# Gate and up products with half of the tokens stationary and 512 weight columns moving

## The chip, the cores and the metric

The kernel runs on one core of one Trainium2 chip. The metric is the device time of one execution in microseconds (us), and the kernel before is given by three such times. Beside them stands one profiled execution, whose trace gives every instruction's start and duration on the core's engines: TensorE (PE, with its weight loads as PEld), VectorE (DVE), ScalarE (ACT), GpSimd (POOL), and the queue of SyncE (SP), which only issues transfers.

## What is computed

The reference is a causal trunk of two layers on 256 tokens of 1024 features in fp32. Each layer is a half-weighted SwiGLU block, a mixer, and another such block. The mixer is attention with pooling in layer 0 and a state-space layer (S5) with a gated linear unit (GLU) in layer 1. The four SwiGLU blocks (FFN 0 to 3) are what the change touches:

```
def _swiglu(h, w_gate, w_up, w_down):          # 1024 -> 2816 -> 1024
    return (jax.nn.silu(h @ w_gate) * (h @ w_up)) @ w_down

def reference(x, ...):
    for layer in range(2):
        x = x + 0.5 * _swiglu(_rmsnorm(x, ffn_norm[layer, 0]), ...)
        h = _rmsnorm(x, mix_norm[layer])
        x = x + (_even_mixer(h, ...) if layer % 2 == 0 else _odd_mixer(h, ...))
        x = x + 0.5 * _swiglu(_rmsnorm(x, ffn_norm[layer, 1]), ...)
    return x
```

## The kernel before

An fp32 product is made as three products in the type fp32r: high part by high part, high by low, low by high (`mm3`). The transposed, normed input of a block lies on chip as `hTh` and `hTl` (high and low, 8 tiles of 128 features by 256 tokens). Weights come from memory in pieces of 512 KB (tile `raw`, at most 4 on their way) and are split on chip: ACT rounds a piece to its high part (`wh`, `hi_of`, L176) and DVE subtracts that from the piece (`wl`, `tt`, L133). Two pieces make a unit, and 4 units have room at a time.

An FFN walks over 11 groups (`NG`) of 256 of its 2816 inner columns. Its units are ("g", f, g) for gate, ("u", f, g) for up, ("d", f, g) for down. For groups 1 to 10, `gate_up(f, g)` keeps a block of 128 weight columns stationary and moves all 256 tokens: 2 sides (gate, up) by 2 blocks of columns by 8 blocks of features by 3 products are 96 products of 256 columns. Their sums come out with the inner columns on the partitions, which is how the down products want them. So `sg` (Silu, ACT), `pr` (gate times up, DVE), `hh` (high, ACT) and `hl` (low, DVE), each of 128x512, follow straight on:

```
p = wk((128, 2, 256))
i = mm3(p[:, m], w[0][:, k, s], w[1][:, k, s], hTh[:, k], hTl[:, k], k == 0, k == 7)
```

Group 0 of each FFN is made in the head, beside the norm of the tokens' second half, by `gate_up_half`: half of the tokens (128) stationary, 256 weight columns of one side moving. There the sums have tokens on the partitions, so `hid_T` turns the result of a half with two transposes on TensorE (`tr`, 128x128 fp32, into a `sk` tile of PSUM) before `hh` and `hl` are made.

`down(f, g, t, c)` keeps 128 tokens of `hh` or `hl` stationary and moves 512 columns of the down weights, into `acc` tiles of PSUM; a group has 24 such products. `ffn_joint` runs the down products of group g - 1 behind the gate and up products of group g, and the last two groups' stand in `tail`. Outside a few stretches a scheduler, which works before the launch, lays down each engine's order; `prio(CHAIN)` prefers an instruction and `behind(...)` puts it behind others. The program is FFN 0, the mixer of layer 0, FFN 1, FFN 2, S5 with its GLU, FFN 3.

The tables of S5 are built by a generator (`s5_build`) on DVE beside the groups of FFN 1 and FFN 2; the names `X`, `E`, `b_q`, `b_pw`, `b_st` are its tiles. Four loads of 1 MB (`K`, units of kind "K") and four of 512 KB (`rawW`, kind "W") bring S5's maps back on chip when S5 begins, and 16 stores `V<-h` rearrange its input; all of these are issued by SP, in its order.

Of the kernel before, what the change touches and what calls it, by code (L numbers as in the profile page):

```python
# [25 lines left out]
RING = 4        # split units of weights on chip  # L26
RAW = 4         # pieces of weights on their way
CHAIN = 400     # the scheduler's preference for what TensorE waits for
WARM = 32       # products that nothing reads, before S5
WARM0 = 16      # and at the start  # L30
PACE = 0.8      # calls of the generators for a step
# the even mixer, call by call; digits: the half of the tokens and a part, for p the columns, the half (from 6 on of
# the columns, which come out turned) and the part
# h transposes of the input, p projections in, e rotary and rms of queries (0) or keys (1), T their transposes,
# s scores, x exponentials, t transposes of the weights, v values, V their transposes, g sums of windows,
# m their products, G their split, o projections out, l load of a vector
# [5 lines left out]
# S5, two of the eight jq at a time: f front (a copy of the input), u its transposes, w sums of the chunks,  # L42
# s scan, d direct part, o output; h0 transposes of the output's first half, x products that nothing reads
# [8 lines left out]
# columns of the constants: identity, masks of both halves, scales of the first sums of windows, places of d, frequencies  # L52
# [9 lines left out]
def shape_constants():  # L62
# [8 lines left out]
    # the patterns that hold a key, as the logarithm of their number (over the scale of the scores)  # L71
# [3 lines left out]
    # the first sums of a window of w hold fewer than w values  # L75
# [8 lines left out]
class InOrder:  # L84
    """an engine whose instructions keep the order of the program while strict is set"""
# [19 lines left out]
def trunk_kernel(ctx: ExitStack, tc: tile.TileContext, I, out):  # L105
# [19 lines left out]
    # pieces of weights on their way, units split, the step traced, calls due to the generators, units held back  # L125
    state = {"dma": 0, "split": 0, "step": 0, "credit": 0.0, "hold": False}

# [16 lines left out]
    def strict(on):  # L144
        """from here on TensorE keeps the order of the program, or no longer"""
        def f():
            PE.strict = on
        return f
# [17 lines left out]
    @contextmanager  # L166
    def behind(*names):
        """what is traced within is issued behind the instructions kept by these names, each on its engine"""
        with ExitStack() as st:
            for n in names:  # L170
                for i in pins.get(n, ()):
                    st.enter_context(tc.issue_after(i.ins))
            yield
# [20 lines left out]
    def unit_source(uid):  # L194
        kind = uid[0]
        if kind == "g":
            return cols_unit(I["ffn_w_gate"][uid[1] // 2, uid[1] % 2], uid[2])
        if kind == "u":
            return cols_unit(I["ffn_w_up"][uid[1] // 2, uid[1] % 2], uid[2])
# [6 lines left out]
        return cols_unit(I["s5_w_glu"][0], uid[1])  # L206

# [6 lines left out]
    def emit_dma(i):  # L214
# [10 lines left out]
        src, a, b = unit_source(units[i // 2])  # L225
        n = a // 2
        r = wraw.tile([128, n, b], F32, tag="raw", name="raw")
        keep("load", SP.dma_start(out=r, in_=src[:, (i % 2) * n:(i % 2 + 1) * n]))
        raws[i] = r

    def raw_busy(i):
        """whether the room that piece i takes still holds a piece of W"""
# [13 lines left out]
    def split_late():  # L246
        """from here on the low parts wait for split_now()"""
        nonlocal late
        late = []
# [9 lines left out]
    def emit_split(i):  # L259
# [18 lines left out]
        _, a, b = unit_source(units[i])  # L278
        h = wsp.tile([128, a, b], F32R, tag="wh", name="wh")
        l = wsp.tile([128, a, b], F32R, tag="wl", name="wl")  # L280
        n = a // 2
        for p in range(2):
            fill(2 * i + p)
            r = raws.pop(2 * i + p)
            s = slice(p * n, p * n + n)
            with behind(*(["split"] if i + p else ["norm"])):
                hi = hi_of(h[:, s], r)
                if late is None:
                    keep("splits", hi, tt(l[:, s], r, h[:, s].bitcast(F32), ALU.subtract))
                else:  # L290
                    late.append((l[:, s], r, h[:, s].bitcast(F32), ALU.subtract))
# [55 lines left out]
    def table(func, after="square"):  # L347
        """the table of a function, before its first use waits for it"""
# [23 lines left out]
    def split_T(t, kt0, ps):  # L372
        """PSUM [128, 4, 128] -> hi and lo of hT."""
# [13 lines left out]
    hid = {}  # L387

    def gate_up(f, g):
        wg, wu = held["g", f, g], held["u", f, g]  # L390
        ps = []
        for w in (wg, wu):
            p = wk((128, 2, 256))
            for m in range(2):
                for k in range(8):
                    s = slice(m * 128, (m + 1) * 128)
                    i = mm3(p[:, m], w[0][:, k, s], w[1][:, k, s], hTh[:, k], hTl[:, k], k == 0, k == 7)
            ps.append(p)
            if w is wg:
                keep("gate", i)  # L400
        sg = tmp.tile([128, 2, 256], F32, tag="t512", name="sg")
        pr = tmp.tile([128, 2, 256], F32, tag="t512", name="pr")
        h = hidp.tile([128, 2, 256], F32R, tag="hh", name="hh")
        l = hidp.tile([128, 2, 256], F32R, tag="hl", name="hl")
        with prio(CHAIN):
            ACT.activation(out=sg, in_=ps[0], func=AF.Silu)
            tt(pr, sg, ps[1], ALU.mult)
            hi_of(h, pr)
            tt(l, pr, h.bitcast(F32), ALU.subtract)
        hid[f, g] = (h, l)  # L410
# [5 lines left out]
    def gate_up_half(f, g, t, which, ks):  # L416
        w = held["gu"[which], f, g]
# [3 lines left out]
        p = gups[f, g, t][:, which]  # L421
        for x, y in ((hTh, w[0]), (hTh, w[1]), (hTl, w[0])):
            for k in ks:
                keep("gu", mm(p, x[:, k, o], y[:, k], k == 0 and y is w[0] and x is hTh, k == 7 and x is hTl))
        if which == 0 or ks[-1] != 7:
            return
        ps = gups.pop((f, g, t))
# [7 lines left out]
    def hid_T(f, g, t):  # L435
# [7 lines left out]
        with prio(CHAIN), behind("gate" if t else "gu"):  # L443
# [15 lines left out]
    cst = I["cst"]  # L459

# [1 line left out]
    at = {}  # L462

    def even_open():
# [18 lines left out]
        # values to pool and sums of windows, with room for the 8 zeros before the first  # L483
# [20 lines left out]
    def proj_in(c, t, ks):  # L504
        """the projections c of half t, or, where they are pooled, half t of their columns, turned"""
# [26 lines left out]
    def angle_tables(pool, ang, n, cos, sin, name):  # L532
        """cos and sin of ang [128, n]; quadrants by parts of pi / 2 that keep the products exact."""
# [41 lines left out]
        # u = 1 - o ; sin' = s * u + c * o ; cos' = c * u + s * o  # L575
# [670 lines left out]
    def ffn_joint(f, g0, g1, pend):  # L1246
        """groups g0 .. g1 - 1 of both halves; pend: calls that follow the first of them"""
        for g in range(g0, g1):
            paced.add(len(steps))
            S(lambda g=g: gate_up(f, g), ("g", f, g), ("u", f, g))  # L1250
            for fn in pend:
                S(fn)
# [295 lines left out]
```

## Time and profile before

| what | value |
|---|---|
| three runs | 957.85, 960.83, 962.18 us (median 960.83) |
| profiled execution, span from first to last instruction | 960.5 us |
| PE busy | 938.2 us, 98% of the span |
| weight loads (PEld) busy | 870.5 us, 91% |
| DVE busy | 640.9 us, 67% |
| ACT busy | 424.6 us, 44% |
| POOL busy | 58.3 us, 6% |
| mean granted TensorE clock | 0.994 of full speed |
| moved by DMA | 185.47 MB, mean 193 GB/s |

The profiled execution has no time of its own beside its span; the span is 0.33 us below the median of the three runs. Busy shares are means over stages that differ: DVE is lightly loaded in FFN 0 and full beside parts of FFN 1 and FFN 2. A matmul's duration in the trace holds its passage through the array, so consecutive ones overlap, and how long one holds the queue is the difference between two starts.

### The profile page before, as it was taken

The page shows a single profiled execution, that of the slowest core. Times are in us where ns is not written, and L with a number is a line of the kernel's source. Part 1 is how long each engine was busy: PE and PEld are TensorE (multiplying, and loading weights), DVE is VectorE, ACT ScalarE, POOL GpSimd, SP SyncE. Part 2 cuts the span into 40 slices and gives each one's busy share as a digit, 9 for nine tenths or more (in the row PEclk, how much of TensorE's full clock was granted, in tenths as well). Part 3 has the DMA queues.
Part 4 walks back from the last instruction along what each step waited for, and adds up shares of the span by engine and source line. Part 5 has one row for each costly group of instructions (what it writes and reads, how often), then busy time and mean ns, then how long its engine had stood idle before and what let it go on. Part 6 is the DMA issues. An engine that isn't in the chain of part 4 may idle for free.

```text
span 960.5 us, 17371 instructions
## 1 busy us (share of the span) xinstructions
PE 938.2 (98%) x7148; PEld 870.5 (91%) x7148; DVE 640.9 (67%) x1017; ACT 424.6 (44%) x563; POOL 58.3 (6%) x105
## 2 busy tenths in 40 slices
PE   8999999999998999999999999999879999999998
PEld 6999999989987999999999999999659999999997
DVE  5646654488866799997675898844586575554452
ACT  6534433455635443444454443442525364433440
POOL 0000000013020000013100340000000000000000
PEclk9999999999999999999999999999999999999999
DMA  8867666645477664679756696667656457666641
GB/s 246 267 192 227 191 178 198 187 139 163 144 160 221 191 190 147 195 244 298 236 187 181 161 275 182 194 196 249 217 198 208 143 162 218 192 177 195 181 149 44
DMA packets 146047, 185.47 MB, mean 193 GB/s; under 512 B 18896, under 2 KB 128400, under 8 KB 145200
## 3 DMA queue, kind: packets, MB, share of 16 engines
q1 hardware_dynamic: 142720, 175.97, 60.4%
q0 software_dynamic: 3248, 8.39, 3.2%
q8 instruction: 56, 0.92, 0.4%
q14 instruction: 23, 0.19, 0.1%
HBM read 173.85 MB, written 9.44 MB: 191 GB/s over the span
## 4 chain that ended last, share of the span: by engine, by line
PE 86%; DVE 7%; DMA 3%; POOL 1%; issue 1%; ACT 1%; SPq 1%; POOLq 0%; ACTq 0%; DVEq 0%
PE wk L95 56%; PE acc L95 25%; PE sk L95 5%; DVE wl L133 1%; DMA gvec<-in_ffn_norm_dram 1%; DMA V<-h 1%; POOL r L615 1%; DVE h L142 1%; DVE hTl L133 1%; DVE rot L133 1%; DVE G L1131 1%; DVE G L133 1%; DVE h L133 0%; DVE qk L133 0%; POOL rstd L358 0%
## 5 line engine op out<-in xcount | busy, mean ns | idle before, releaser
L176 ACT ACTIVATE wh<-raw 128x1024 fp32r<-128x1024 f32 x304 | 314.6, 1055 | 388.4 <-issue 234.6
L133 DVE TENSOR_TENSOR wl<-raw,wh 128x1024 fp32r<-128x1024 f32 x304 | 366.7, 1224 | 166.8 <-ACT wh L176 165.7
L95 PE MATMUL wk<-hTh,wh 128*128 128x256 f32 x1312 | 368.8, 284 | 0.1
L95 PE MATMUL wk<-hTh,wl 128*128 128x256 f32 x1312 | 367.9, 283 | 0.0
L95 PE MATMUL wk<-hTl,wh 128*128 128x256 f32 x1312 | 367.9, 283 | 0.0
L95 PEld LDWEIGHTS wk<-hTh,wh 128*128 128x128 f32 x1312 | 250.1, 192 | 2.3 <-DVE qk L133 0.6
L95 PEld LDWEIGHTS wk<-hTl,wh 128*128 128x128 f32 x1312 | 250.2, 192 | 1.4
L95 PEld LDWEIGHTS wk<-hTh,wl 128*128 128x128 f32 x1312 | 250.2, 192 | 0.0
L95 PE MATMUL acc<-wh,hh 128*128 128x512 f32 x352 | 138.3, 393 | 0.0
L95 PE MATMUL acc<-wl,hh 128*128 128x512 f32 x352 | 137.7, 391 | 0.0
L95 PE MATMUL acc<-wh,hl 128*128 128x512 f32 x352 | 137.2, 390 | 0.0
L95 PEld LDWEIGHTS acc<-wh,hl 128*128 128x128 f32 x352 | 66.2, 188 | 14.2 <-DVE hl L133 0.3
L95 PEld LDWEIGHTS acc<-wh,hh 128*128 128x128 f32 x352 | 66.3, 188 | 12.9 <-issue 0.4
L95 PEld LDWEIGHTS acc<-wl,hh 128*128 128x128 f32 x352 | 66.3, 188 | 12.1
L133 DVE TENSOR_TENSOR pr<-sg,wk 128x512 f32<-128x512 f32 (+1 forms) x48 | 30.8, 643 | 68.0 <-PE wk L95 51.0
L95 PE MATMUL wk<-wh,hTh 128*128 128x256 f32 x288 | 57.2, 293 | 0.3 <-ACT hTh L176 0.3
L95 PE MATMUL wk<-wh,hTl 128*128 128x256 f32 x288 | 55.4, 287 | 1.2 <-DVE hTl L133 1.2
L95 PE MATMUL wk<-wl,hTh 128*128 128x256 f32 x288 | 55.9, 288 | 0.1
L95 PEld LDWEIGHTS wk<-wh,hTh 128*128 128x128 f32 x288 | 44.6, 196 | 1.4 <-ACT hTh L176 0.5
L95 PEld LDWEIGHTS wk<-wh,hTl 128*128 128x128 f32 x288 | 44.0, 195 | 1.6 <-DVE hTl L133 1.6
L95 PEld LDWEIGHTS wk<-wl,hTh 128*128 128x128 f32 x288 | 44.1, 195 | 0.4 <-DVE wl L133 0.3
L358 POOL TENSOR_TENSOR rstd<-ss,mhalf 128x1 f32<-128x1 f32 x12 | 7.5, 624 | 399.9 <-DVE ss L142 399.9
(280 smaller groups left out, 761.0 us busy)
## 6 DMA issues: line engine op xcount, KB each, us to landing
raw<-in_ffn_w_gate_dram SPq DMA_DIRECT2D x88, 512.0 KB
raw<-in_ffn_w_up_dram SPq DMA_DIRECT2D x88, 512.0 KB
raw<-in_ffn_w_down_dram SPq DMA_DIRECT2D x88, 512.0 KB
raw<-in_ev_w_in_dram SPq DMA_DIRECT2D x16, 512.0 KB
raw<-in_s_w_glu_dram SPq DMA_DIRECT2D x16, 512.0 KB
raw<-in_ev_w_out_dram SPq DMA_DIRECT2D x8, 512.0 KB
K<-dK SPq DMA_DIRECT2D x4, 1024.0 KB
dK<-E POOLq DMA_DIRECT2D x36, 64.0 KB, 5.0
```

What stands on the lines that cost most here:

```text
L95: i = f(*a, **k)
L133: return DVE.tensor_tensor(out=o, in0=a, in1=b, op=op)
L142: return DVE.scalar_tensor_tensor(out=o, in0=a, scalar=s, in1=b, op0=op0, op1=op1)
L176: return ACT.activation(out=o, in_=i, func=AF.Copy)
L358: POOL.tensor_tensor(out=rstd, in0=ss[:, 2:3], in1=mhalf, op=ALU.pow)
L615: POOL.tensor_tensor(out=r8, in0=s8, in1=mhalf.to_broadcast([128, 8]), op=ALU.pow)
L1131: i = DVE.tensor_tensor_scan(out=v, data0=s5["R"][:, k], data1=v, initial=0.0, op0=ALU.mult, op1=ALU.add)
```

## The change

Every group now goes the way of the head, with wider moving blocks. A unit ("f", f, g, kh) holds 512 of the 1024 features (half kh) of both gate and up, 256 columns of each side by side: its two pieces are a gate piece and an up piece of 512 KB, as large as before. `gate_up(f, g, t, kh, ks)` keeps 128 tokens stationary and moves 512 weight columns (256 of gate and 256 of up) into one bank of PSUM; a group has 48 of these products, two halves of tokens by two halves of features by 4 blocks by 3. Behind the second half of features come `sg` and `pr` of 128x256 for that half of the tokens, and `hid_T` with its two transposes makes its part of `hh` and `hl`. `ffn_joint` places `HID(f, g, 0)` between the two feature halves of the tokens' second half, and `HID(f, g - 1, 1)` between those of the first half of the next group. The first call of FFN 0 is made side by side, 24 products of 256 columns. All else in the file is lines whose comments are gone.

```diff
+    def pieces(uid):
+        if uid[0] == "f":
+            f, g, kh = uid[1:]
+            return (4, 2, 256), [
+                (I[nm][f // 2, f % 2, kh * 512:(kh + 1) * 512, g * 256:(g + 1) * 256].rearrange("(k p) f -> p k f", p=128),
+                 (slice(None), slice(None), q)) for q, nm in enumerate(("ffn_w_gate", "ffn_w_up"))]
+        src, a, b = unit_source(uid)
+        n = a // 2
+        return (a, b), [(src[:, q * n:(q + 1) * n], (slice(None), slice(q * n, (q + 1) * n))) for q in range(2)]
...
-        _, a, b = unit_source(units[i])
-        h = wsp.tile([128, a, b], F32R, tag="wh", name="wh")
-        l = wsp.tile([128, a, b], F32R, tag="wl", name="wl")
-        n = a // 2
+        shape, places = pieces(units[i])
+        h = wsp.tile([128, *shape], F32R, tag="wh", name="wh")
+        l = wsp.tile([128, *shape], F32R, tag="wl", name="wl")
         for p in range(2):
             fill(2 * i + p)
             r = raws.pop(2 * i + p)
-            s = slice(p * n, p * n + n)
+            s = places[p][1]
             with behind(*(["split"] if i + p else ["norm"])):
-                hi = hi_of(h[:, s], r)
+                hi = hi_of(h[s], r)
                 if late is None:
-                    keep("splits", hi, tt(l[:, s], r, h[:, s].bitcast(F32), ALU.subtract))
+                    keep("splits", hi, tt(l[s], r, h[s].bitcast(F32), ALU.subtract))
                 else:
-                    late.append((l[:, s], r, h[:, s].bitcast(F32), ALU.subtract))
+                    late.append((l[s], r, h[s].bitcast(F32), ALU.subtract))
...
-    def gate_up(f, g):
-        wg, wu = held["g", f, g], held["u", f, g]
-        ps = []
-        for w in (wg, wu):
-            p = wk((128, 2, 256))
-            for m in range(2):
-                for k in range(8):
-                    s = slice(m * 128, (m + 1) * 128)
-                    i = mm3(p[:, m], w[0][:, k, s], w[1][:, k, s], hTh[:, k], hTl[:, k], k == 0, k == 7)
-            ps.append(p)
-            if w is wg:
-                keep("gate", i)
-        sg = tmp.tile([128, 2, 256], F32, tag="t512", name="sg")
-        pr = tmp.tile([128, 2, 256], F32, tag="t512", name="pr")
-        h = hidp.tile([128, 2, 256], F32R, tag="hh", name="hh")
-        l = hidp.tile([128, 2, 256], F32R, tag="hl", name="hl")
-        with prio(CHAIN):
-            ACT.activation(out=sg, in_=ps[0], func=AF.Silu)
-            tt(pr, sg, ps[1], ALU.mult)
-            hi_of(h, pr)
-            tt(l, pr, h.bitcast(F32), ALU.subtract)
-        hid[f, g] = (h, l)
...
-    def gate_up_half(f, g, t, which, ks):
-        w = held["gu"[which], f, g]
+    def gate_up(f, g, t, kh, ks):
+        w = held["f", f, g, kh]
         o = slice(t * 128, (t + 1) * 128)
         if (f, g, t) not in gups:
             gups[f, g, t] = wk((128, 2, 256))
-        p = gups[f, g, t][:, which]
-        for x, y in ((hTh, w[0]), (hTh, w[1]), (hTl, w[0])):
-            for k in ks:
-                keep("gu", mm(p, x[:, k, o], y[:, k], k == 0 and y is w[0] and x is hTh, k == 7 and x is hTl))
-        if which == 0 or ks[-1] != 7:
+        ps = gups[f, g, t]
+        sides = [slice(0, 1), slice(1, 2)] if (f, g, t, kh) == (0, 0, 0, 0) else [slice(0, 2)]
+        for sd in sides:
+            for x, y in ((hTh, w[0]), (hTh, w[1]), (hTl, w[0])):
+                for k in ks:
+                    keep("gu", mm(ps[:, sd], x[:, 4 * kh + k, o], y[:, k, sd],
+                                  kh == 0 and k == 0 and y is w[0] and x is hTh and sd.start == 0,
+                                  kh == 1 and k == 3 and x is hTl))
+        if kh == 0 or ks[-1] != 3:
             return
-        ps = gups.pop((f, g, t))
+        del gups[f, g, t]
...
-        with prio(CHAIN), behind("gate" if t else "gu"):
+        with prio(CHAIN), behind("down" if t and g == NG - 1 else "gu"):
...
+    def GU(f, g, t, kh, *qs):
+        for ks in [(2 * q, 2 * q + 1) for q in qs] or [(0, 1, 2, 3)]:
+            S(lambda ks=ks: gate_up(f, g, t, kh, ks), ("f", f, g, kh))
...
+    def HID(f, g, t):
+        S(lambda: hid_T(f, g, t))
+    def ffn_joint(f, g0, g1):
         for g in range(g0, g1):
             paced.add(len(steps))
-            S(lambda g=g: gate_up(f, g), ("g", f, g), ("u", f, g))
-            for fn in pend:
-                S(fn)
-            pend = ()
+            GU(f, g, 0, 0)
+            HID(f, g - 1, 1)
+            GU(f, g, 0, 1)
+            GU(f, g, 1, 0)
+            HID(f, g, 0)
+            GU(f, g, 1, 1)
             if g < NG - 1:
                 for t in range(2):
                     dn(f, g - 1, t)
@@ -1258,6 +1252,7 @@
     def tail(f, fin_a, fin_b):
         S(strict(f == 1))
         dn(f, NG - 2, 0)
+        HID(f, NG - 1, 1)
...
-        for n in range(3):
-            GU(f, 0, n // 2, n % 2)
+        GU(f, 0, 0, 0, 0, 1)
+        GU(f, 0, 0, 1, 0)
         S(lambda: h_transpose(1, sk, "gu"))
         S(release)
-        GU(f, 0, 1, 1)
-        for n in range(4):
-            GU(f, 1, n // 2, n % 2)
-        S(lambda: hid_T(f, 0, 0))
+        GU(f, 0, 0, 1, 1)
+        for n in range(2):
+            GU(f, 0, 1, n, 0, 1)
+        HID(f, 0, 0)
...
     GU(0, 0, 0, 0)
-    GU(0, 0, 0, 1)
-    GU(0, 0, 1, 0)
     S(lambda: h_transpose(1))
     S(lambda: table(AF.Silu, "hT"))
-    GU(0, 1, 0, 0)
-    GU(0, 1, 0, 1)
+    GU(0, 0, 1, 0)
+    GU(0, 0, 0, 1)
     GU(0, 0, 1, 1)
-    GU(0, 1, 1, 0)
-    GU(0, 1, 1, 1)
-    S(lambda: hid_T(0, 0, 0))
-    ffn_joint(0, 1, 4, (lambda: hid_T(0, 0, 1),))
+    HID(0, 0, 0)
+    ffn_joint(0, 1, 4)
```

On TensorE, in the middle of FFN 0, a group before is a run of 256-column products with weights stationary, and then the down products (behind the arrow stands the moving tile and then the stationary one); the last rows of the one and the first of the other:

```order
L95 MATMUL wk<-hTh,wh 128x256
L95 MATMUL wk<-hTl,wh 128x256
L95 MATMUL wk<-hTh,wl 128x256
L95 MATMUL acc_470<-wh,hh 128x512
L95 MATMUL acc_470<-wl,hh 128x512
L95 MATMUL acc_470<-wh,hl 128x512
L95 MATMUL acc_470<-wh,hh 128x512
```

After the change the same place reads, from the transposes of the group before, which stand behind the first 12 products, to the first down product:

```order
L95 MATMUL sk<-ident,pr 128x128 x2
L95 MATMUL wk<-wh,hTh 128x512 x4
L95 MATMUL wk<-wl,hTh 128x512 x4
L95 MATMUL wk<-wh,hTl 128x512 x4
L95 MATMUL wk<-wh,hTh 128x512 x4
L95 MATMUL wk<-wl,hTh 128x512 x4
L95 MATMUL wk<-wh,hTl 128x512 x4
L95 MATMUL sk<-ident,pr 128x128 x2
L95 MATMUL wk<-wh,hTh 128x512 x4
L95 MATMUL wk<-wl,hTh 128x512 x4
L95 MATMUL wk<-wh,hTl 128x512 x4
L95 MATMUL acc_393<-wh,hh 128x512
```

The 96 products of 256 columns have become 4 times 12 of 512, with two pairs of transposes among them: the first pair is that of the group before (its second half of tokens), the second that of this group's first half.

On DVE, in a group of FFN 1 beside which the tables of S5 are turned (`E<-X`, `b_st<-X`), before:

```order
L133 TENSOR_TENSOR wl<-raw,wh 128x1024 x2
L901 STREAM_TRANSPOSE b_st<-X 128x256 x2
L133 TENSOR_TENSOR wl<-raw,wh 128x1024 x2
L901 STREAM_TRANSPOSE E<-X 128x256 x4
L133 TENSOR_TENSOR pr<-sg,wk 128x512
L133 TENSOR_TENSOR wl<-raw,wh 128x1024
L133 TENSOR_TENSOR hl<-pr,hh 128x512
L133 TENSOR_TENSOR wl<-raw,wh 128x1024
```

And after the change, at the same calls of the generator:

```order
L133 TENSOR_TENSOR wl<-raw,wh 128x4x256 x2
L889 STREAM_TRANSPOSE b_st<-X 128x256
L133 TENSOR_TENSOR hl<-sk,hh 128x2x128
L889 STREAM_TRANSPOSE b_st<-X 128x256 x3
L133 TENSOR_TENSOR pr<-sg,wk 128x256
L889 STREAM_TRANSPOSE E<-X 128x256
L133 TENSOR_TENSOR wl<-raw,wh 128x4x256
L133 TENSOR_TENSOR hl<-sk,hh 128x2x128
L133 TENSOR_TENSOR wl<-raw,wh 128x4x256
L133 TENSOR_TENSOR pr<-sg,wk 128x256
L889 STREAM_TRANSPOSE E<-X 128x256
L133 TENSOR_TENSOR wl<-raw,wh 128x1024 x2
```

The products `pr` of a group and the low parts `hl` are now two each, of half the size, and stand among the splits `wl` and the generator's instructions at two places of the group in place of one.

On SP's queue, where S5 begins, before:

```order
L265 DMA K_7188<-dK 128x2048
L265 DMA K_7189<-dK 128x2048
L1034 DMA hTh<-dW 128x2048
L1034 DMA hTl<-dW 128x2048
L265 DMA K_7192<-dK 128x2048
L1021 DMA V<-h_85 16x8x128 x6
L1021 DMA V<-h_86 16x8x128 x4
L1021 DMA V<-h_85 16x8x128 x2
L1021 DMA V<-h_86 16x8x128 x4
L222 DMA rawW<-dW 128x1024 x4
L265 DMA K_7193<-dK 128x2048
```

And after:

```order
L271 DMA K_5949<-dK 128x2048
L1022 DMA hTh<-dW 128x2048
L1022 DMA hTl<-dW 128x2048
L271 DMA K_5948<-dK 128x2048
L1009 DMA V<-h_85 16x8x128 x6
L1009 DMA V<-h_86 16x8x128 x4
L1009 DMA V<-h_85 16x8x128 x2
L1009 DMA V<-h_86 16x8x128 x4
L271 DMA K_5975<-dK 128x2048
L229 DMA rawW<-dW 128x1024 x4
L271 DMA K_5976<-dK 128x2048
```

The two loads of the table K that were issued first are now one, with the second behind the loads `hTh` and `hTl`. The third now stands behind the stores `V<-h` and ahead of the loads `rawW`.

## Rows read from the trace of the kernel before

**Rows 1.** page, part 1: busy us (share of the span) and instructions

```profile
PE 938.2 (98%) x7148; PEld 870.5 (91%) x7148; DVE 640.9 (67%) x1017; ACT 424.6 (44%) x563; POOL 58.3 (6%) x105
```

**Rows 2.** page, part 4: chain that ended last, share of the span by line

```profile
PE wk L95 56%; PE acc L95 25%; PE sk L95 5%; DVE wl L133 1%; DMA gvec<-in_ffn_norm_dram 1%; DMA V<-h 1%; POOL r L615 1%; DVE h L142 1%; DVE hTl L133 1%; DVE rot L133 1%; DVE G L1131 1%; DVE G L133 1%; DVE h L133 0%; DVE qk L133 0%; POOL rstd L358 0%
```

**Rows 3.** chain in FFN 0: start us, us, what

```profile
94.54 11.51 PE wk L95 x96
106.05 5.47 PE acc L95 x24
```

**Rows 4.** timeline of PE in FFN 0: start us, us, instruction, count

```profile
107.27 0.39 PE L95 MATMUL acc<-wh,hh 128*128 128x512 f32 x1
...
111.13 0.39 PE L95 MATMUL acc<-wh,hl 128*128 128x512 f32 x1
```

**Rows 5.** timeline of PE in the head of FFN 1

```profile
308.77 0.64 PE L95 MATMUL wk<-wh,hTl 128*128 128x256 f32 x4
309.25 0.38 PE L95 MATMUL sk<-ident,pr 128*128 128x128 f32 x2
...
309.58 0.28 PE L95 MATMUL wk<-hTl,wh 128*128 128x256 f32 x1
```

**Rows 6.** chain in the head of FFN 3

```profile
780.82 0.22 PE sk L95 x2
```

**Rows 7.** instructions on tile pr: duration ns min/median/max, starts

```profile
L95 PE MATMUL sk<-ident,pr x16: 271/273/273, 26.0 to 786.7; 128*128 128x128 f32 x16
```

**Rows 8.** windows: us, busy PE PEld DVE ACT POOL, PEclk, DMA, GB/s

```profile
77.56:94.54 16.98, 16.98 (x122) 16.02 (x122) 10.14 (x24) 7.03 (x8) 0.00 (x0) 1.00 0.85 249
412.18:429.16 16.98, 16.98 (x123) 16.02 (x122) 16.98 (x25) 7.38 (x8) 4.29 (x8) 1.00 0.74 228
556.54:573.52 16.98, 16.98 (x123) 16.02 (x122) 16.98 (x24) 7.15 (x8) 8.32 (x16) 1.00 0.91 275
```

**Rows 9.** chain and timeline of DVE, end of a group of FFN 1

```profile
423.70 5.47 PE acc L95 x24
...
424.40 1.43 DVE L901 STREAM_TRANSPOSE E<-X 128x256 f32<-128x256 f32 x4
425.74 0.66 DVE L133 TENSOR_TENSOR pr<-sg,wk 128x512 f32<-128x512 f32 x1
426.31 1.22 DVE L133 TENSOR_TENSOR wl<-raw,wh 128x1024 fp32r<-128x1024 f32 x1
```

**Rows 10.** timelines of ACT and DVE in the head of FFN 2

```profile
499.07 0.38 ACT L431 ACTIVATE sg<-wk 128x256 f32<-128x256 f32 x1 [0.82 <-PE wk L95]
499.62 2.01 ACT L176 ACTIVATE wh<-raw 128x1024 fp32r<-128x1024 f32 x2
...
499.61 0.41 DVE L133 TENSOR_TENSOR pr<-sg,wk 128x256 f32<-128x256 f32 x1
499.94 0.42 DVE L133 TENSOR_TENSOR hl<-sk,hh 128x256 fp32r<-128x256 f32 x1
```

**Rows 11.** timeline of SP where S5 begins

```profile
664.09 0.82 SPq L265 DMA_DIRECT2D K<-dK  x2
...
690.88 2.33 SPq L222 DMA_DIRECT2D rawW<-dW  x4
693.30 0.69 SPq L265 DMA_DIRECT2D K<-dK  x1
```

**Rows 12.** timeline of PE in S5, with idle time before and releaser

```profile
698.35 0.86 PE L95 MATMUL sk<-rawW,U 128*32 128x128 f32 x24 [0.56 <-DMA rawW<-dW]
...
700.06 0.63 PE L95 MATMUL sk<-ident,Sb 128*128 128x128 f32 x4
```

**Rows 13.** chain in S5

```profile
703.22 0.60 DVE h L133
```

**Rows 14.** timeline of PE ahead of S5: products that nothing reads

```profile
680.68 7.08 PE L95 MATMUL wk<-warm 128*128 128x512 bf16 x32
687.60 0.60 PE L95 MATMUL acc<-warm 128*128 128x256 bf16 x4
```

More of the change, by code (lines that the diff above doesn't have):

```diff
@@ L195, in unit_source @@
         kind = uid[0]
[L196 to L199, printed above, removed]
         if kind == "d":
@@ L224, in emit_dma @@
             return
-        src, a, b = unit_source(units[i // 2])
-        n = a // 2
-        r = wraw.tile([128, n, b], F32, tag="raw", name="raw")
-        keep("load", SP.dma_start(out=r, in_=src[:, (i % 2) * n:(i % 2 + 1) * n]))
+        src = pieces(units[i // 2])[1][i % 2][0]
+        r = wraw.tile(list(src.shape), F32, tag="raw", name="raw")
+        keep("load", SP.dma_start(out=r, in_=src))
         raws[i] = r
@@ L277, in emit_split @@
             return
-        _, a, b = unit_source(units[i])
-        h = wsp.tile([128, a, b], F32R, tag="wh", name="wh")
-        l = wsp.tile([128, a, b], F32R, tag="wl", name="wl")
-        n = a // 2
+        shape, places = pieces(units[i])
+        h = wsp.tile([128, *shape], F32R, tag="wh", name="wh")
+        l = wsp.tile([128, *shape], F32R, tag="wl", name="wl")
         for p in range(2):
@@ L1234, in drain @@
         gens.clear()
-    def GU(f, t, which, q):
-        S(lambda: gate_up_half(f, 0, t, which, range(4 * q, 4 * q + 4)), ("gu"[which], f, 0))
+    def GU(f, g, t, kh, *qs):
+        for ks in [(2 * q, 2 * q + 1) for q in qs] or [(0, 1, 2, 3)]:
+            S(lambda ks=ks: gate_up(f, g, t, kh, ks), ("f", f, g, kh))
     def dn(f, g, t, cs=(0, 1)):
@@ L1244, in dn @@
             S(lambda c=c: down(f, g, t, c), ("d", f, g))
-    def ffn_joint(f, g0, g1, pend):
+    def HID(f, g, t):
+        S(lambda: hid_T(f, g, t))
+    def ffn_joint(f, g0, g1):
         for g in range(g0, g1):
             paced.add(len(steps))
-            S(lambda g=g: gate_up(f, g), ("g", f, g), ("u", f, g))
-            for fn in pend:
-                S(fn)
-            pend = ()
+            GU(f, g, 0, 0)
[4 more added lines that the diff above has]
+            GU(f, g, 1, 1)
             if g < NG - 1:
@@ L1356, in trunk_kernel @@
     S(opened)
-    ffn_joint(0, 4, NG, ())
+    ffn_joint(0, 4, NG)
     tail(0, N(0, "m0"), HT(0))
@@ L1404, in trunk_kernel @@
     S(lambda: gens.append(s5_build()))
-    ffn_joint(1, 1, NG, (lambda: hid_T(1, 0, 1),))
+    ffn_joint(1, 1, NG)
     S(lambda: load_g("f2", I["ffn_norm"][1, 0]))
@@ L1410, in trunk_kernel @@
     head(2, "f2")
-    ffn_joint(2, 1, 8, (lambda: hid_T(2, 0, 1),))
+    ffn_joint(2, 1, 8)
     S(drain)
     S(s5_run_open)
-    ffn_joint(2, 8, NG, ())
+    ffn_joint(2, 8, NG)
     S(lambda: load_g("m1", I["mix_norm"][1]))
@@ L1490, in trunk_kernel @@
     head(3, "f3")
-    ffn_joint(3, 1, NG, (lambda: hid_T(3, 0, 1),))
+    ffn_joint(3, 1, NG)
     for t in range(2):
         dn(3, NG - 2, t)
+        if t == 0:
+            HID(3, NG - 1, 1)
         for c in range(2):
```

## The prediction

> **What bounds the kernel now.** First the busy shares: PE is busy for 98% of the span, DVE for 67%, ACT for 44% [rows 1]. Such shares mix stages, so next the chain of work that ended last, by line: gate, up and projection products (wk) are 56% of the span, down products (acc) 25%, the rest small [rows 2]. In FFN 0 the chain holds PE alone: 96 gate and up products take 11.51 us, 24 down products 5.47 us, and the next block starts where the last one ended [rows 3]. So a group costs 16.98 us, without a hole, and there are 40 such groups (10 in each of 4 FFNs): 679 us. Third, what one product holds of PE's queue. 17 intervals of 512 columns lie between 107.27 and 111.13 us: 227.1 ns each [rows 4]; over a whole block, 5470 / 24 = 227.9 ns. A product of 256 columns takes 11510 / 96 = 119.9 ns [rows 3]. Two of 256 columns thus cost 239.8 ns and one of 512 costs 227.1, as if each product carried some 13 ns whatever its width. Last, the windows: the clock is 1.00, DVE works 10.14 of 16.98 us in a quiet group and all of it in groups that share it with the building of S5's tables [rows 8]. PE sets the pace even there, since its stretch has no hole either.
>
> **The change, part by part.** *Products.* A group's 96 x 119.9 = 11.51 us become 48 x 227.1 = 10.90 us, a gain of 0.61. The trace of before has no gate product of 512 columns with tokens stationary. The nearest rows are the down products: the same type, 128 tokens stationary and loaded anew for each product, 512 weight columns moving from split weights, PSUM as target. I take their 227.1. Products with tokens stationary stand in the heads: four of 256 columns from 308.77 to 309.25, 120 ns each [rows 5], so which side is stationary costs nothing. Bounds: from 216.3 ns (32 bf16 products of 512 columns in 6.92 us [rows 14]) to 239.8 ns (no fixed part saved).
>
> *Transposes.* Before, group 0 alone had them; now each group has two pairs. A pair starts at 309.25, and the second product behind it at 309.58; with one product's 0.12 taken off, 0.21 us [rows 5]; the chain of another head gives 0.22 [rows 6]. I take 0.217. Two pairs: +0.43 per group. Lower bound 0.42; upper bound each of four at its whole duration of 0.273 [rows 7], 1.09.
>
> *Down products.* Unchanged in number; they no longer follow 256-column ones, so 24 x 227.1 = 5.45 in place of 5.47.
>
> A group: 10.90 + 0.43 + 5.45 = 16.78 against 16.98, or -0.20; with 227.9 ns everywhere -0.14, with 226.7 -0.23. Times 40: **-8.0 us** (-5.6 to -9.2).
>
> *Group 0.* It had its transposes before, so the whole 11.51 - 10.90 = 0.61 is gained in three FFNs: -1.8. FFN 0 keeps 24 narrow products: 24 x 0.120 + 36 x 0.227 = 11.05, -0.5. Together **-2.3**.
>
> *ACT.* It gets two Silu and two `hh` of 0.38 us per group [rows 10] for one each of twice the size: some 0.4 us more at most, in a group where it works 7.03 of 16.98 [rows 8]. Hidden by its idle time.
>
> *DVE.* Products and low parts of 256 columns hold its queue for 0.33 us (499.61 to 499.94 [rows 10]), those of 512 for 0.57 (425.74 to 426.31 [rows 9]): 4 x 0.33 - 2 x 0.57 = +0.18 per group. In quiet groups nearly 7 us of idle time hide it.
>
> *The new wait.* Before, `pr`, `hh` and `hl` had the next group's 11.51 us to be ready. Now TensorE's transposes of a group's first half stand only 12 products behind the end of that half's sums: 12 x 0.227 = 2.72 us. In that time Silu and product must be made. From the start of `sg` to the start of `pr` is 0.54 us, `pr` takes 0.41 [rows 10]; with an estimated 0.2 for the signals on both sides 1.15 us. That leaves 1.6 us. Behind the transposes wait 12 gate products and then the down products, all in order. In quiet groups DVE is reached at once. In a full one I read the lateness from the old `pr`: the gate and up products ended at 423.70, behind `E<-X` `pr` began at 425.74, 2.04 us later [rows 9]. The same lateness now would end `pr` at 2.04 + 0.41 = 2.45, just inside 2.72. Windows 412.18 and 556.54 stand for about seven groups in which DVE has no idle time; some will come later than that one, because a `wl` (1.22) may stand ahead too. I put 1.2 us on all seven; bounds nothing and 1 us each, 7. The second half's transposes have 5.45 + 2.72 = 8.2 us of cover, enough everywhere.
>
> *Transfers and splits.* Pieces, bytes and splits keep their size. The first unit's room is now free 2.7 us before the end of the group's products rather than at their half (5.8 before). The unit that takes it is read first behind the down products and a quarter of the next group: 2.7 + 5.45 + 2.72 = 10.9 us later, and its splits take two wh (2.01 on ACT [rows 10]) and two wl of 1.22 on DVE [rows 9], 4.5 at most. Hidden. Where S5 begins, SP's order moves: of two K loads issued together at 664.09 one goes behind `hTh` and `hTl`, and the third goes behind the stores, ahead of the four `rawW` loads of 690.88 [rows 11]. That puts 1 MB in front of `rawW`; at the 275 GB/s of a busy window [rows 8] 3.8 us. `rawW` was already late: 24 products waited 0.56 us for it at 698.35 [rows 12]. Behind these hang the transposes that end at 700.7, and DVE uses them at 703.22 on the chain [rows 12, 13]: 2.5 us of slack. So 3.8 - 2.5 = 1.3 at worst, nothing at best if the queues carry the loads side by side; I take 0.3. POOL's order stays as it was.
>
> Sum: 960.5 - 8.0 - 2.3 + 1.2 + 0.3 = 951.7 us of span. The median of the runs is 0.3 above the span, so **952.0 us**.
>
> **A rule against the change.** The rows say that a second product costs some 13 ns beside its columns. The Trainium skill, page "TensorE: Matmul & The Clock Gate", section "Back-to-back issue gap", gives a warm gap of N / 2.4 + 2.5 ns, so that joining two products would save only 2.5 ns; by that figure a 512-column product would cost 237.3 ns, a group 0.31 us more than before, and the whole about 974 us. The bf16 rows of this trace, 216.3 ns [rows 14], agree with its formula, the fp32r rows of 227.1 [rows 4] do not.
>
> **Rivals.** *A: as forecast*, 949 to 955.
>
> *B: DVE's full groups hold TensorE.* For it: DVE works 16.98 of 16.98 us there and gets 0.18 more while the group gets 0.20 shorter. Against: its lateness of 2.04 still fits, and wl is made ahead for units that are read much later. At 1 us in each of seven groups, 952.0 - 1.2 + 7 = 958; it ends as no change.
>
> *C: the wide product saves nothing* (other side). Place: the 48 products of each group; price 239.8 ns each. Then a group costs 11.51 + 0.43 + 5.47 = 17.41, +0.43; times 40, with nothing from group 0 and 1.5 for the waits: 979 us. It decides at (11.51 - 0.43) / 48 = 231 ns. Against: the 227.1 of the down products [rows 4]; for: a different pattern of writes into one bank, which no row shows. The skill's formula is the milder form of this rival.
>
> *D: transposes at their whole duration* (other side too). 1.09 per group rather than 0.43, +0.66 x 40 = +26: 978 us; it decides when a pair costs 0.32 or more. Against: rows 5 and 6, where a pair took 0.21 and 0.22. The Trainium skill, page "TensorE: Matmul & The Clock Gate", section "Part 4: PE-mode transpose", gives about 275 ns for one in a kernel. The trace's duration of 273 ns agrees with that, but a pair holds the queue for less than one.
>
> *E: the wide product runs at bf16's 216.3 ns.* 48 x 10.8 = 0.52 less per group, 43 groups: 22 us, 930 us. Against: no fp32r row comes near it.
>
> *F: the Silu, product and transposes chain isn't covered in quiet groups.* A wait of 0.25 us in each of 40 groups brings 962, no change. Against: 1.6 us of slack.
>
> **How the numbers follow.** A 0.70, B 0.15, C 0.05 (the formula's form included), D 0.03, E 0.03, F 0.04. A measurement of this kernel tells about 0.5%, 4.8 us, from no change; the runs of before lie 4.3 apart. Faster, below 956.0: all of A, E, and a third of B: 0.78. Same: the rest of B and most of F, with the edge of C: 0.15. Slower, above 965.6: C, D and a little of F: 0.07. The range takes A and B: below, the bound of -9.2 with no wait at all (960.5 - 9.2 - 2.3 + 0.3 = 949.3) less 0.8 for the scatter of three runs, 948.5; above, B's 958 and 1 for the same scatter, 959. C, D, E and F, 0.15, lie outside, with a little of B.
>
> **What would show it.** In the trace of after: starts of wk products of 512 columns 226 to 228 ns apart in a group's interior; 0.21 to 0.22 us around each pair of transposes; a quiet group of 16.75 to 16.82 us against 16.98; no idle time of PE ahead of transposes in FFN 0 and FFN 3, and less than 0.5 us in any group of FFN 1 and 2; S5's start no more than 1.3 us longer. The prediction fails if wide gate products start 231 ns or more apart, if a pair costs 0.32 us or more, or if PE waits for `pr` over 5 us in all.

## The result, and the profile after

The changed kernel takes 970.49 us (median of 4 runs, 968.98 to 971.64), the kernel before 961.22 (median of 4). The ratio is 1.0096, with a 95% interval of 1.0073 to 1.0118: the change made the kernel about 9 us slower. The forecast was 952.0, in a range of 948.5 to 959.0.

The profiled execution has a span of 969.9 us, 9.4 more than before. Its page, part 1, and from part 4 the chain that ended last by engine and by line:

```profile
PE 932.9 (96%) x5208; PEld 773.9 (80%) x5208; DVE 645.0 (67%) x1097; ACT 436.1 (45%) x643; POOL 58.3 (6%) x105
...
PE 70%; DVE 15%; DMA 6%; issue 3%; ACT 3%; POOL 1%; SPq 1%; POOLq 0%; DVEq 0%; ACTq 0%
PE wk L95 43%; PE acc L95 21%; PE sk L95 6%; DVE wl L133 4%; DMA raw<-in_ffn_w_up_dram 3%; DVE X L133 2%; DMA gvec<-in_ffn_norm_dram 1%; ACT wh L176 1%; DVE b_q L133 1%; POOL r L603 1%; DVE h L142 1%; DVE pr L133 1%; DVE b_t L133 1%; DVE hTl L133 1%; DVE rot L133 1%
```

TensorE has 5 us less work than in [rows 1] and yet the span is longer, so it waits some 15 us more. Of the chain, the gate, up and projection products (wk) held 56% and now hold 43% [rows 2]; in their place stand DVE's splits and tables, and transfers of weights. What TensorE waits for, by the list of its waits (us in total, times, longest). Two entries stand out against before, where the list has no wait for `pr`, and 1.5 us for a copy of h on ACT where now a copy on DVE costs 5.6; the waits for the norms' `h` (L142), 8.0 before, are 10.0.

```profile
PE sk L95 <- DVE pr L133: 6.8, 6, 1.8
PE wk L95 <- DVE h L1033: 5.6, 1, 5.6
```

In a quiet group of FFN 0 the chain reads (start us, us, what; it answers to [rows 3]):

```profile
88.67 5.44 PE acc L95 x24
94.11 2.72 PE wk L95 x12
96.83 0.22 PE sk L95 x2
97.05 5.50 PE wk L95 x24
102.55 0.22 PE sk L95 x2
102.77 2.77 PE wk L95 x12
```

The down products begin at 88.67 and the next group's at 105.54, 16.87 us later; before it was 16.98. That is a gain of 0.11, where 0.20 was forecast. In FFN 1 and most of FFN 2 a group without a hole takes 16.81.

To see where 9.4 us arise, the starts of the same products are compared (after less before, on the timelines of PE): first down product of FFN 1, -1.43 (319.76 against 321.19); first of FFN 2, +1.52 (512.34 against 510.82); the products that nothing reads ahead of S5, +3.42 (684.10 against 680.68 [rows 14]); first of FFN 3, +10.09 (802.69 against 792.60); the end, +9.4. So FFN 1 lost 2.95, FFN 2 lost 1.90, and the stretch from S5 to FFN 3's first down product lost 6.67. FFN 0 and FFN 3, the quiet stretches, gained.

**S5.** The timelines of ACT, DVE and PE where S5 begins:

```profile
691.94 0.40 ACT L1031 COPY h<-V 128x256 f32<-128x256 f32 x1 [4.68 <-DMA V<-h]
692.25 3.89 ACT L176 ACTIVATE wh<-raw 128x1024 fp32r<-128x1024 f32 x4
...
693.34 3.50 DVE L133 TENSOR_TENSOR wl<-raw,wh 128x1024 fp32r<-128x1024 f32 x3 [5.13 <-ACT wh L176]
696.75 0.29 DVE L1033 COPY h<-V 128x256 f32<-128x256 f32 x1
...
697.18 0.66 PE L95 MATMUL wk<-ident,h 128*128 128x128 f32 x2 [5.56 <-DVE h L1033]
698.40 1.94 PE L95 MATMUL sk<-hTh,U 128*32 128x128 f32 x32
```

Four splits `wh` of GLU weights now stand behind ACT's copy of h, which waits 4.68 us for the transfer V<-h. Behind the splits hang three `wl` on DVE, and behind these, in DVE's order, the other copy of h that S5's first transposes need. Before, ACT made the splits first, from 683.75 on, in the time in which it had to wait for V anyway (timelines of ACT and PE in the kernel before):

```profile
683.75 3.88 ACT L176 ACTIVATE wh<-raw 128x1024 fp32r<-128x1024 f32 x4
689.23 0.40 ACT L1043 COPY h<-V 128x256 f32<-128x256 f32 x1 [1.60 <-DMA V<-h]
...
690.64 1.08 PE L95 MATMUL sk<-hTh,U 128*32 128x128 f32 x32 [0.34 <-DVE U L1066]
```

The windows of the idle stretch in the changed kernel and of the 6.1 us behind it (columns as in [rows 8], PEclk third from the end):

```profile
691.60:697.20 5.60, 0.04 (x2) 0.05 (x1) 3.70 (x4) 4.20 (x5) 0.00 (x0) 0.82 0.63 190
697.20:703.30 6.10, 5.96 (x78) 4.63 (x79) 1.56 (x2) 2.72 (x8) 0.00 (x0) 0.61 0.96 371
```

TensorE, idle for 5.6 us, was granted a clock of 0.61 in the stretch behind, part of it at the lower level of 1.2 GHz. The 32 products sk<-hTh,U took 1.94 us; in the kernel before, with the clock at 1.00, they took 1.08.

**A hole ahead of transposes.** The chain in a group of FFN 2:

```profile
555.77 7.83 DMA raw<-in_ffn_w_up_dram
...
564.71 1.23 DVE wl L133
...
568.68 0.34 DVE pr L133
...
569.07 0.44 PE sk L95 x2
```

A piece of up weights landed late; the split `wl` waited for it, with it all that stands behind it on DVE, an `hl` (0.34) and four table instructions (0.6 each), and at their end `pr`, for which the transposes and so all of TensorE waited.

### The profile page after: what moved, and what is told of

Same layout as the page of the kernel before. It is cut to its first block, busy times and chain, and to the rows that moved or that the text cites. A ratio compares the mean times of both kernels' runs of the same rounds, so it can differ in the third digit from the quotient of the medians.

```text
span 969.9 us, 13624 instructions
## 1 busy us (share of the span) xinstructions
PE 932.9 (96%) x5208; PEld 773.9 (80%) x5208; DVE 645.0 (67%) x1097; ACT 436.1 (45%) x643; POOL 58.3 (6%) x105
## 4 chain that ended last, share of the span: by engine, by line
PE 70%; DVE 15%; DMA 6%; issue 3%; ACT 3%; POOL 1%; SPq 1%; POOLq 0%; DVEq 0%; ACTq 0%
PE wk L95 43%; PE acc L95 21%; PE sk L95 6%; DVE wl L133 4%; DMA raw<-in_ffn_w_up_dram 3%; DVE X L133 2%; DMA gvec<-in_ffn_norm_dram 1%; ACT wh L176 1%; DVE b_q L133 1%; POOL r L603 1%; DVE h L142 1%; DVE pr L133 1%; DVE b_t L133 1%; DVE hTl L133 1%; DVE rot L133 1%
## 5 line engine op out<-in xcount | busy, mean ns | idle before, releaser
L95 PE MATMUL wk<-wh,hTh 128*128 128x512 f32 (+1 forms) x868 | 235.4, 382 | 0.3 <-ACT hTh L176 0.3
L95 PE MATMUL wk<-wh,hTl 128*128 128x512 f32 (+1 forms) x868 | 226.0, 371 | 1.2 <-DVE hTl L133 1.2
L95 PE MATMUL wk<-wl,hTh 128*128 128x512 f32 (+1 forms) x868 | 226.1, 371 | 0.5 <-DVE wl L133 0.5
L95 PEld LDWEIGHTS wk<-wh,hTl 128*128 128x128 f32 x868 | 158.6, 189 | 29.8 <-DVE hTl L133 1.6
L95 PEld LDWEIGHTS wk<-wl,hTh 128*128 128x128 f32 x868 | 158.7, 189 | 29.6 <-DVE wl L133 0.9
L95 PEld LDWEIGHTS wk<-wh,hTh 128*128 128x128 f32 x868 | 152.0, 190 | 22.5 <-ACT hTh L176 0.5
L419 ACT ACTIVATE sg<-wk 128x256 f32<-128x256 f32 x88 | 33.7, 382 | 114.5 <-PE wk L95 114.5
L133 DVE TENSOR_TENSOR pr<-sg,wk 128x256 f32<-128x256 f32 x88 | 36.7, 417 | 65.2 <-ACT sg L419 65.1
L133 DVE TENSOR_TENSOR hl<-sk,hh 128x256 fp32r<-128x256 f32 x88 | 36.7, 417 | 10.8 <-ACT hh L176 10.8
L95 PE MATMUL sk<-ident,pr 128*128 128x128 f32 x176 | 34.0, 275 | 6.8 <-DVE pr L133 6.8
L142 DVE SCALAR_TENSOR_TENSOR h<-x,rstd,gvec 128x512 f32<-128x512 f32 (+1 forms) x25 | 17.2, 727 | 17.6 <-DMA gvec<-in_ffn_norm_dram 11.4
```

The lines of the kernel that those rows point to most:

```text
L95: i = f(*a, **k)
L133: return DVE.tensor_tensor(out=o, in0=a, in1=b, op=op)
L142: return DVE.scalar_tensor_tensor(out=o, in0=a, scalar=s, in1=b, op0=op0, op1=op1)
L419: ACT.activation(out=sg, in_=ps[:, 0], func=AF.Silu)
```

## The experiments

All ratios are to the kernel before, run on the same chip, and intervals are of 95%.

**S5's order on ACT alone.** The four splits are kept by a name, and S5's first copies stand behind it:

```diff
                 else:
+                    keep("yhi", hi)
                     late.append((l[s], r, h[s].bitcast(F32), ALU.subtract))
...
-        with prio(CHAIN), behind("late" if k == 0 else "U0" if k == 1 else f"Sb{k - 2}"):
+        with prio(CHAIN), behind(*(("late", "yhi") if k == 0 else ("U0",) if k == 1 else (f"Sb{k - 2}",))):
```

> The changed kernel, with one tie more: where S5 begins, ACT copies h out of V only behind the four splits wh of the GLU weights, as it did before the change. Theory A (the lost order on ACT): the changed kernel's idle time of TensorE ahead of S5's first transposes, 5.6 us, falls to the 1.5 of before, the clock doesn't fall with it, and the whole is 5 to 6.5 us shorter, 964 to 965.5. Rival B (the K load that moved ahead of the rawW loads, and the rawW loads behind it, set the start of S5): the idle time moves to the rawW products, and the whole is within 2 us of the changed kernel, 968.5 or more.

963.10 us, ratio 1.0009 (0.9994 to 1.0025): 0.87% or 8.4 us less than the changed kernel's 1.0096. That is more than expected, but the two intervals together leave some 6 to 11 us, which reaches the expected 6.5. The timelines of ACT and PE:

```profile
688.11 3.88 ACT L176 ACTIVATE wh<-raw 128x1024 fp32r<-128x1024 f32 x4
692.90 0.40 ACT L1032 COPY h<-V 128x256 f32<-128x256 f32 x1 [0.91 <-ACT wh L176]
...
693.29 0.41 PE L95 MATMUL wk<-ident,h 128*128 128x128 f32 x2 [0.73 <-ACT h L1032]
694.26 1.08 PE L95 MATMUL sk<-hTh,U 128*32 128x128 f32 x32 [0.35 <-DVE U L1055]
...
703.63 0.43 PE L95 MATMUL sk<-rawW,U 128*32 128x128 f32 x8 [1.24 <-DMA rawW<-dW]
704.78 0.86 PE L95 MATMUL sk<-rawW,U 128*32 128x128 f32 x24 [0.72 <-DMA rawW<-dW]
```

The idle time is 0.73 and the 32 products take 1.08 again. From the start of the products that nothing reads (685.05) to FFN 3's first down product (796.68) it is 111.6 us; the changed kernel needed 118.6, the kernel before 111.9. Theory A stands. The moved loads show, as rival B had it, in the waits for rawW (1.24 and 0.72, before 0.56 [rows 12]), but no loss of time shows there. The hole ahead of transposes in FFN 3's first full group, also behind a late piece of up weights, is shorter: 0.5 us by the list of waits, 1.3 in the changed kernel. With one each of FFN 0, FFN 1 and FFN 2 the list has 6.0 us in 4. A hole can cost more than itself: in this profiled execution, the longest of the ten, FFN 2's is 2.5 us, and from 569.20 to 572.70, right behind it, the granted clock was 0.51, nearly all of it at the lower level of 1.2 GHz; eight wide products took 3.24 us there in place of 1.83.

**The same order put into the kernel before.** Here ACT's first copy is made ahead of the splits, which stand behind it; DVE's order stays:

```diff
-    def s5_front(k):
+    def s5_front(k, gs=(0, 1)):
...
-            for g in range(2):
+            for g in gs:
...
-                    ACT.copy(out=o, in_=i)
+                    keep(f"h{k}", ACT.copy(out=o, in_=i))
...
     def ahead():
+        s5_front(0, (1,))
         release("square")
+        pins["split"] = pins["h0"]
         split_late()
...
-    S(lambda: s5_front(0))
+    S(lambda: s5_front(0, (0,)))
```

> The kernel before, with only ACT's order at the start of S5 turned round as the changed kernel has it: the first copy of h out of V ahead of the four splits wh of the GLU weights. Theory A (this order costs the changed kernel its 6 us in S5): 5 to 6.5 us slower than before, 966 to 967.5, with TensorE idle for 5 us or more ahead of S5's first transposes. Rival B (the moved loads on SP do it): within 1.5 us of before.

967.49 us, ratio 1.0059 (1.0044 to 1.0074): 5.7 us slower, without one wide product. The timelines of ACT and PE show the changed kernel's picture:

```profile
689.78 0.40 ACT L1043 COPY h<-V 128x256 f32<-128x256 f32 x1 [4.80 <-DMA V<-h]
690.09 3.89 ACT L176 ACTIVATE wh<-raw 128x1024 fp32r<-128x1024 f32 x4
...
695.02 0.66 PE L95 MATMUL wk<-ident,h 128*128 128x128 f32 x2 [5.68 <-DVE h L1045]
```

**The first half's transposes later.**

```diff
-            HID(f, g, 0)
             GU(f, g, 1, 1)
+            HID(f, g, 0)
```

> The changed kernel, with the transposes of a group's first half moved behind the last products of the group, so that they have 24 products (5.45 us) of cover rather than 12 (2.72). Theory A (the cover is too short where pr stands late in DVE's queue): the seven holes ahead of transposes in the groups of FFN 1, 2 and 3, 7.0 us together, nearly go, and the whole is 5 to 7 us shorter, 963.5 to 965.5; the 1.0 us hole of FFN 0's first group, whose place isn't moved, stays. Rival B (DVE and the weight pieces are the bound in those groups): the holes reappear later in the same groups, and the whole stays above 968.

962.39 us, ratio 1.0010 (0.9999 to 1.0020): 8.3 us less than the changed kernel, somewhat more than expected, but with intervals that reach the expectation. The list of waits keeps S5's (5.6) and hardly any for `pr`:

```profile
PE sk L95 <- DVE pr L133: 0.3, 1, 0.3
```

DVE has as much to do as in the changed kernel, and no new wait has come up in those groups: the groups that took up to 18.88 us take 16.81 to 17.02. In the group of FFN 2 that had the longest hole `pr` is even later here. In the changed kernel the products behind the half's sums begin at 564.34 and `pr` at 568.60, 4.26 us later; here it is 5.13 us, and the transposes follow without a hole (PE, DVE, PE):

```profile
559.59 1.07 PE L95 MATMUL wk<-wh,hTh 128*128 128x512 f32 x4
...
564.72 0.41 DVE L133 TENSOR_TENSOR pr<-sg,wk 128x256 f32<-128x256 f32 x1
...
565.19 0.44 PE L95 MATMUL sk<-ident,pr 128*128 128x128 f32 x2
```

So it was the cover that was short, and DVE and the pieces are not the bound at this pace; rival B falls. FFN 0's hole, whose place isn't moved, is 0.3 us here by the list (0.9 in the changed kernel), and a quiet group of FFN 3 takes 16.81 in place of 16.87; neither was expected.

**No transposes.**

```diff
-        ps = sk((128, 2, 128))
-        with prio(CHAIN), behind("down" if t and g == NG - 1 else "gu"):
-            for m in range(2):
-                tr(ps[:, m], pr[:, m * 128:(m + 1) * 128], ident)
+        ps = pr.rearrange("p (m n) -> p m n", m=2)
+        with prio(CHAIN):
             hi_of(h, ps)
```

> The changed kernel without hid_T's transposes: hh and hl are made from pr itself, so the down products multiply results that aren't turned; all else is as in the changed kernel. It gives what a pair of transposes costs in the stream of wide products. Theory A (a pair costs 0.27 us in all, 0.14 for the two and the rest in the products behind it, which run at 227 ns otherwise): a quiet group takes 10.90 + 5.45 = 16.35 us instead of 16.87, that is 21 us over 40 groups, and with the holes ahead of transposes gone (8 us) the whole is about 941. Rival B (a pair costs the forecast 0.217, and the wide products themselves are dearer in this kernel, 229 ns): a quiet group takes 16.44, and the whole is 944 to 946.

941.85 us, ratio 0.9795 (0.9772 to 0.9819). The chain in FFN 0:

```profile
89.91 10.88 PE wk L95 x48
100.79 5.44 PE acc L95 x24
```

48 wide products in 10.88 us are 226.7 ns each, as the down products. A group takes 16.32; with two pairs it takes 16.87 or 16.81, so a pair costs (16.87 - 16.32) / 2 = 0.275 us, or 0.245. Theory A stands, at the upper of the two. The pair itself is 0.22 in the chain above; the rest is in the products behind it (24 in 5.50 where 24 x 226.7 are 5.44). In two groups of FFN 1 TensorE waits here for the split `wl` itself, so late pieces can hold it up without transposes:

```profile
PE wk L95 <- DVE wl L133: 1.8, 2, 1.4
```

**Both repairs.** The edits of the first and third experiment together.

> The changed kernel with both repairs: ACT's order at the start of S5, and the transposes of a group's first half behind the group's last products. Theory A (the two losses are separate and add): 8.4 us from the one and 8.3 from the other, by the ratios of the single runs to the kernel before, leave a ratio of about 0.992, 953 to 955 us, faster than before. Rival B (a common cause, such as late weight pieces, that shows up at either place): no better than the better of the two single repairs, a ratio of 1.000.

957.71 us, ratio 0.9955 (0.9939 to 0.9971): faster than before, and better than either repair alone, so rival B falls. The gain is short of the 0.992 that was expected if the two add, by 0.0032; the intervals leave about as much open, and what either repair takes off FFN 3's hole is counted twice in the 0.992. The chain in FFN 0 (start us, us, what):

```profile
105.81 5.47 PE acc L95 x24
111.28 2.73 PE wk L95 x12
114.01 0.22 PE sk L95 x2
114.22 8.18 PE wk L95 x36
122.40 0.22 PE sk L95 x2
```

A pair that stands right ahead of the down products costs 0.22 and some 0.03 behind it; the group takes 16.81. The profiled execution (span 952.9) is the shortest of nine, which lie between 954.64 and 959.41, and shows no hole ahead of transposes but one of 1.0 us. What the longer executions lose isn't seen. One thing that varies is the group itself: it takes 16.81 in some stretches and 16.87 in others (here in FFN 2), which over 40 groups is up to 2.4 us.

**All four transposes in one place.** Both halves' calls of `HID` for group g - 1 stand behind the first 12 products of group g, in heads and tails likewise; ACT's order is repaired as above.

```diff
             GU(f, g, 0, 0)
+            HID(f, g - 1, 0)
             HID(f, g - 1, 1)
             GU(f, g, 0, 1)
             GU(f, g, 1, 0)
-            HID(f, g, 0)
             GU(f, g, 1, 1)
```

> The changed kernel with ACT's order at the start of S5 repaired, and all four transposes of a group in one place, behind the first 12 products of the next group: 8.2 us of cover, and one interruption of the wide products per group instead of two. Theory A (an interruption costs the two starts of 0.14 for each pair and once some 0.14 in the products behind it): 0.41 per group in place of 0.55, so 5 us less than with the transposes at two places, 948 to 950. Rival B (each pair carries its own 0.27 wherever it stands): the same as with both repairs and two places, 953 to 955.

955.00 us, ratio 0.9925 (0.9907 to 0.9944), the fastest of the kernels that compute the whole, 7.2 us below before. The chain in FFN 3:

```profile
791.89 2.72 PE wk L95 x12
794.61 0.44 PE sk L95 x4
795.05 8.19 PE wk L95 x36
803.23 5.44 PE acc L95 x24
```

A group takes 16.79 nearly everywhere, so four joined transposes cost 16.79 - 16.32 = 0.47, neither the 0.41 of A nor B's 0.55, and only 0.02 less than two pairs with the second ahead of the down products. The 948 to 950 of A is missed: joining saves little, and the start that A gave it, an additive 953 to 955, was already too low.

**The moved load of K behind rawW.** In the joined version both loads of the second K table are held back until the rawW loads are issued:

```diff
-            load(0)
             if n:
-                s5["more"] = lambda: load(1)
+                s5["more"] = lambda: (load(0), load(1))
             else:
+                load(0)
                 load(1)
```

> The version with joined transposes and ACT's order repaired, and in addition the K load that the change had moved ahead of the four rawW loads now behind them. Theory A (the scan on DVE covers the late rawW, as the forecast's 0.3 us for the moved loads had it): TensorE's waits for rawW, 1.8 us in the version without this edit, fall to 0.6 or less, and the whole gains at most 1 us, a ratio to the kernel before of 0.991 to 0.993. Rival B (the late rawW sets S5's pace once the order on ACT is repaired): 2 to 3 us, a ratio of 0.990 or less.

955.32 us, ratio 0.9936 (0.9916 to 0.9955): no different from the joined version within the intervals (A's 0.991 to 0.993 lies inside them, B's 0.990 outside). The wait for rawW, 1.8 us there, is no longer in the list of waits; one for K stands in it:

```profile
PE acc L95 <- DMA K<-dK: 0.6, 1, 0.6
```

Theory A stands in that nothing is gained. In this version's chain S5 is nearly all DVE's work, its scans among it. In the joined version a load rawW (7.35 us) stands on the chain, and the whole takes no longer; that DVE's scan covers it, as A had it, isn't shown beyond that.

## Why the prediction was wrong

The step that failed is the claim that the change lays nothing else on the path, in two places: the term of 0.3 us for S5, and the 1.2 us for the new wait. By the profiled executions they were 5.2 (the 6.67 of that stretch less FFN 3's hole, 1.44) and 8.0. Signs of being wrong that it had named came: TensorE waited over 5 us for `pr`, FFN 0 and FFN 3 have a hole each, and a quiet group takes 16.87, not 16.75 to 16.82.

*Wide products: right.* 226.7 ns without transposes, 227.1 forecast; 96 narrow ones in 11.51 us became 48 in 10.88. Rivals C and E fall. The Trainium skill's page "TensorE: Matmul & The Clock Gate", section "Back-to-back issue gap", gives a formula for an isolated product's gap, by which one of 512 columns takes 2.5 ns less than two of 256. Here two of 256 take 239.8 [rows 3] and one of 512 takes 226.7, 13.1 ns less, and the measurement decides.

*Transposes: mis-sized.* A pair costs 0.245 to 0.275 us among wide products, where 0.217 was read among narrow ones [rows 5, 6]. The row that gave it was right for its place (0.22 stands in the chain of after too), and it holds the first product behind the pair, which took 0.20 (309.38 to 309.58) where 0.12 is usual. What it lacked is that among wide products those behind the first run late as well, some 0.04 us in all in the rows of the last section. In the groups of FFN 0 and FFN 3 two pairs cost 0.12 more than forecast, in the others 0.06. Rival D, each at its whole 0.273, falls.

*Group: -0.11 or -0.17 rather than -0.20.* Taken as 20 groups of each, that is -5.6 in place of -8.0.

*The new wait: rival B's size, by another path.* Rival F falls, since quiet groups have no hole but for the first ones of FFN 0 and FFN 3. B's size, 7 us, nearly came out, but by luck: B had DVE without idle time. Instead an engine stood idle shortly ahead of each of the seven holes, for a load: a piece of weights in six, one for S5's tables in the seventh. In the chain of FFN 2 above DVE had idled 2.07 us ahead of the `wl`. In two groups of FFN 1 the delay came by ACT, where `sg` stood behind a `wh` that waited for its piece (ACT and DVE):

```profile
400.56 1.06 ACT L176 ACTIVATE wh<-raw 128x1024 fp32r<-128x1024 f32 x1 [2.14 <-DMA raw<-in_ffn_w_up_dram]
...
401.92 0.42 DVE L133 TENSOR_TENSOR pr<-sg,wk 128x256 f32<-128x256 f32 x1 [1.24 <-ACT sg L419]
```

The argument put the old lateness of `pr`, 2.04 us [rows 9], beside a cover of 2.72 and found room. It left out that `pr` stands behind a `wl`, or its `sg` behind a `wh`, which waits for a piece; when one is late, the transposes are. Start to start, less a product's own 0.227, the holes ahead of transposes are 1.0, 0.25 and 1.7 us in FFN 1, 0.5 and 2.0 in FFN 2, 1.4 in FFN 3 and 1.0 in FFN 0: 8.0 in all (6.8 by the list of waits, which counts from modelled ends). That the cover decides was shown by moving the transposes. Where each piece's lateness comes from was only read from the chains.

*S5: not in the forecast at all.* The moved loads on SP were priced at 0.3, and the experiment with K behind rawW shows no cost of theirs (0.3 is less than it can tell). What cost the time was ACT's order: four splits that had stood ahead of a copy came to stand behind it. The forecast argued from PE's and SP's order at this place, and from ACT's inside the FFNs alone. The repair in the changed kernel and the reversal in the kernel before show the cause from both sides: 8.4 us and 5.7 us. The difference lies within what the intervals leave, about 3; FFN 3's hole, 0.8 us shorter with the repair, is part of it.

*Left over.* The stretch of S5 was forecast 0.5 shorter (0.3 for the loads, -0.6 and -0.2 for FFN 3's first two groups) and is 5.2 longer without the hole: 5.7 more. The holes are 6.8 more, the groups 2.4. Ahead of FFN 2's head TensorE waits 1.2 us for a norm whose weights (gvec) were issued behind a late piece. Together 16.1 of the 18.2 us between the forecast span of 951.7 and 969.9; the rest, some 2, isn't put down to anything.

## What to carry to other kernels

A change that alters the order in which a scheduler sees the work can cost its time in a stage that it doesn't touch. Compare each engine's order over the whole program, above all at the boundaries, where an instruction that waits for a transfer holds up whatever is queued behind it. When a result that had a whole stage of cover gets a short one, add up all that can stand ahead of it in every queue that it passes, not the lateness that was seen while nobody waited. And halving the number of products by widening them is a gain per product, which the transposes that it needs nearly eat up: here 0.63 us gained and 0.47 to 0.55 paid per group.

## What the runs showed of the hardware

A pair of fp32 transposes costs more than the 0.22 us that it holds in the chain: the first four wide products behind it take 1.02 us and the next four 0.92, where four take 0.91 otherwise, as PE's timeline in the changed kernel shows:

```profile
96.67 0.38 PE L95 MATMUL sk<-ident,pr 128*128 128x128 f32 x2
96.81 1.18 PE L95 MATMUL wk<-wh,hTh 128*128 128x512 f32 x4
97.83 1.08 PE L95 MATMUL wk<-wl,hTh 128*128 128x512 f32 x4
98.75 1.08 PE L95 MATMUL wk<-wh,hTl 128*128 128x512 f32 x4
99.66 1.07 PE L95 MATMUL wk<-wh,hTh 128*128 128x512 f32 x4
```

The same group runs at one of two paces, 16.81 or 16.87 us, for whole FFNs at a time; which of them holds differs between kernels and places, and what sets it stays open. The 0.06 lies behind the two pairs: twelve products take 2.85 us in the rows above (96.81 to 99.66), and 2.82 in a group of FFN 2 at the faster pace (597.21 to 600.03).
